# SwiGLU gate and up in Strassen's seven half-size products, with weight sums on GpSimd, in a two-layer encoder trunk

## The chip, the cores and the metric

The kernel runs on one core of one Trainium2 chip. The metric is the device time of one execution in microseconds (us); lower is better. The kernel before takes 2379.37 us (median of 3 runs, 2378.38 to 2380.26).

## The reference

512 tokens of width 1024 go through two layers. Each layer is a half-step SwiGLU, a mixer (gated short convolution beside latent attention), a second half-step SwiGLU and a gated per-layer input; a last RMSNorm follows. All is float32. The part that the change touches is the SwiGLU, of which there are four, each with an inner width of 2816 (22 blocks of 128):

```python
def rmsnorm(x, g):
    y = xf * lax.rsqrt(jnp.mean(xf * xf, axis=-1, keepdims=True) + EPS)
    return (y * g.astype(jnp.float32)).astype(x.dtype)

def swiglu(x, w_gu, w_down):
    g, u = jnp.split(x @ w_gu, 2, axis=-1)
    return (jax.nn.silu(g) * u) @ w_down

for i in range(DEPTH):
    h = h + 0.5 * swiglu(rmsnorm(h, ffn1_norm[i]), ffn1_w_gu[i], ffn1_w_down[i])
    ...
    h = h + merged @ w_o[i]
    h = h + 0.5 * swiglu(rmsnorm(h, ffn2_norm[i]), ffn2_w_gu[i], ffn2_w_down[i])
    ...
```

## The kernel before

**Layout.** The residual stream is eight tiles `h`, each 128 features by 512 tokens. Weights are stationary, activations move. The four SwiGLU stages have the name prefixes a0 and b0 (first layer) and a1 and b1 (second); the mixers are m0 and m1, the per-layer inputs e0 and e1.

**Arithmetic in parts.** Every float32 operand is split into a high part (a cast to fp32r) and a low part (the rest). A product of two tiles takes three matmuls: high by high, high by low, low by high (`mm3`, L155 to L157). A split is a cast on ScalarE and a subtraction on VectorE: for weights L68 and L69 (tiles `wh`, `wl`, 128x1024, eight 128x128 tiles at once), for activations L147/L148, or L150/L151 with the norm's gain folded in.

**Weights.** One DRAM array holds all weight tiles in the order of use. SyncE's queue loads blocks of 16 tiles (1 MB) into three buffers `st`; each block is split in two halves; three buffers each of `wh` and `wl`.

**A SwiGLU stage** (`ffn`). `normed` scales each `h[k]` by the gain, splits it (`x0h`, `x0l`, up to `x7l`) and adds up the squares, on ScalarE and GpSimd (L212 to L216, `acc`). The factor 1/rms is the same for all rows of a token, so the products start without it: `rms` (L225 to L233) multiplies the two parts of `acc` (`ah`, `al`) with ones on TensorE and works out `r` on VectorE (with a reciprocal, L230) and ScalarE (a square root) while the first products run. For each of the 22 blocks f there is a gate product `pg` and an up product `pu`, each 8 x 3 matmuls of 512 columns. Then follow L305 (times r, VectorE from PSUM), L306 (silu, ScalarE), L307 (times r, VectorE), L308 (product of both, GpSimd, or VectorE for the last block of a chunk) and the split. After each chunk of 8, 8 and 6 blocks, eight down products `pd` add that chunk into `h` (L332).

**What sets the order.** The framework puts the instructions of each engine into one fixed list, close to the order of the code, with weight loads and splits moved forward as far as free buffers allow. On the chip each engine works through its list in order and waits at semaphores.

## Time and profile before

| | before |
|---|---|
| timed runs, median (lowest to highest) | 2379.37 us (2378.38 to 2380.26) |
| profiled execution, first to last instruction | 2377.9 us (1.5 us under the median of the runs) |
| mean granted TensorE clock | 0.997 of full speed |
| HBM read, written | 223.66 MB, 2.10 MB |
| first matmuls of a0, b0, a1, b1 start at | 6.8, 771.8, 1186.3, 1944.6 us |
| first matmuls of m0, e0, m1, e1 start at | 369.2, 1131.4, 1546.5, 2304.2 us |

The starts of the stages come from the timeline of TensorE. Each SwiGLU stage thus takes about 360 us. In the profile PE is TensorE's matmuls, PEld its weight loads, DVE VectorE, ACT ScalarE, POOL GpSimd and SP SyncE; a group's row gives its instructions' busy time and the mean of one in nanoseconds, then the idle time of the engine before them and what ended it. L12 is line 12 of the kernel.

### The profile page before, as it was taken

Reading aid. Unit: us, or ns where it says so; the run is one execution under the profiler, and the core shown is the slowest. Engines: PE = TensorE matmul, PEld = TensorE weight load, DVE = VectorE, ACT = ScalarE, POOL = GpSimd, SP = SyncE. Lnnn points to the kernel's source line nnn. Section 1 sums busy time; section 2 is a strip of 40 time slices with the busy share of each in tenths; the row PEclk is TensorE's granted clock in tenths of the full one; section 3 lists DMA queues with packets and bytes.
Section 4 is the critical chain, followed back from the end, with each engine's and each line's share of the span. In section 5 each row is a group of like instructions: output and inputs, shape, how many; then the busy total and the mean of one; then the engine's idle time right before and its main releaser. Section 6 shows DMA issues by size and latency. Waiting matters only on the chain.

```text
span 2377.9 us, 26581 instructions
## 1 busy us (share of the span) xinstructions
PE 2350.9 (99%) x10888; PEld 1967.3 (83%) x10888; DVE 1291.0 (54%) x1735; ACT 832.7 (35%) x1186; POOL 316.2 (13%) x239
## 2 busy tenths in 40 slices
PE   8999999999999999999999999999999999999998
PEld 7888887888888888888888888888888888888888
DVE  6444466754864543435653343467358645444468
ACT  5222234233543322223432222333245333232245
POOL 2000012200222100001310000112012221010011
PEclk9999999999999999999999999999999999999999
DMA  5322222323113232323223232323221132222233
GB/s 178 100 95 93 102 93 89 106 89 101 42 54 107 89 106 89 107 89 115 89 90 106 89 106 89 107 89 107 89 81 47 69 106 89 97 98 91 104 116 124
DMA packets 34537, 227.46 MB, mean 96 GB/s; under 512 B 4080, under 2 KB 4080, under 8 KB 7792
## 3 DMA queue, kind: packets, MB, share of 16 engines
q1 hardware_dynamic: 34128, 225.51, 27.6%
q8 instruction: 85, 1.39, 0.2%
q10 hardware_dynamic: 288, 0.26, 0.0%
q14 instruction: 36, 0.29, 0.0%
HBM read 223.66 MB, written 2.10 MB: 95 GB/s over the span
## 4 chain that ended last, share of the span: by engine, by line
PE 93%; DVE 4%; ACT 1%; issue 1%; POOL 0%; DMA 0%; SPq 0%; ACTq 0%; POOLq 0%; DVEq 0%
PE a0pg L156 2%; PE a0pg L155 2%; PE a1pg L156 2%; PE a0pu L156 2%; PE a0pg L157 2%; PE a0pu L155 2%; PE a0pu L157 2%; PE b1pg L155 2%; PE b1pu L155 2%; PE a1pd L157 2%; PE b0pd L157 2%; PE a1pg L157 2%; PE b0pg L157 2%; PE b0pg L155 2%; PE b0pu L155 2%; PE b0pu L157 2%
## 5 line engine op out<-in xcount | busy, mean ns | idle before, releaser
L69 DVE TENSOR_TENSOR wl<-st,wh 128x1024 fp32r<-128x1024 f32 (+1 forms) x423 | 565.4, 1337 | 392.7 <-ACT wh L68 391.7
L68 ACT CAST wh<-st 128x1024 fp32r<-128x1024 f32 (+1 forms) x423 | 440.8, 1043 | 869.1 <-issue 121.9
L308 POOL TENSOR_TENSOR b0un<-b0un,b0gn 128x512 f32<-128x512 f32 x19 | 25.3, 1333 | 289.4 <-DVE b0un L307 248.7
L308 POOL TENSOR_TENSOR b1un<-b1un,b1gn 128x512 f32<-128x512 f32 x19 | 25.4, 1336 | 288.8 <-DVE b1un L307 250.0
L308 POOL TENSOR_TENSOR a1un<-a1un,a1gn 128x512 f32<-128x512 f32 x19 | 25.3, 1333 | 287.9 <-DVE a1un L307 242.8
L308 POOL TENSOR_TENSOR a0un<-a0un,a0gn 128x512 f32<-128x512 f32 x19 | 25.3, 1333 | 282.1 <-ACT wh L68 166.4
L307 DVE TENSOR_TENSOR a0un<-a0pu,a0r 128x512 f32<-128x512 f32 x22 | 15.2, 690 | 59.5 <-PE a0pu L157 59.5
L307 DVE TENSOR_TENSOR b1un<-b1pu,b1r 128x512 f32<-128x512 f32 x22 | 15.2, 690 | 59.4 <-PE b1pu L157 59.4
L332 DVE SCALAR_TENSOR_TENSOR h<-b1pd,h 128x512 f32<-128x512 f32 x24 | 16.6, 690 | 54.6 <-PE b1pd L157 54.6
L332 DVE SCALAR_TENSOR_TENSOR h<-a0pd,h 128x512 f32<-128x512 f32 x24 | 16.5, 689 | 52.1 <-PE a0pd L157 52.1
L305 DVE TENSOR_TENSOR a0gn<-a0pg,a0r 128x512 f32<-128x512 f32 x22 | 15.2, 691 | 31.5 <-PE a0pg L157 31.4
L305 DVE TENSOR_TENSOR b1gn<-b1pg,b1r 128x512 f32<-128x512 f32 x22 | 15.2, 690 | 31.0 <-PE b1pg L157 31.0
L306 ACT ACTIVATE a1gn<-a1gn 128x512 f32<-128x512 f32 x22 | 13.9, 632 | 47.4 <-DVE a1gn L305 47.4
L306 ACT ACTIVATE b0gn<-b0gn 128x512 f32<-128x512 f32 x22 | 13.9, 632 | 47.4 <-DVE b0gn L305 47.4
L332 DVE SCALAR_TENSOR_TENSOR h<-a1pd,h 128x512 f32<-128x512 f32 x24 | 16.6, 691 | 15.3 <-PE a1pd L157 15.3
L332 DVE SCALAR_TENSOR_TENSOR h<-b0pd,h 128x512 f32<-128x512 f32 x24 | 16.6, 690 | 14.6 <-PE b0pd L157 14.5
L307 DVE TENSOR_TENSOR b0un<-b0pu,b0r 128x512 f32<-128x512 f32 x22 | 15.2, 689 | 10.1 <-PE b0pu L157 10.1
L307 DVE TENSOR_TENSOR a1un<-a1pu,a1r 128x512 f32<-128x512 f32 x22 | 15.2, 689 | 10.1 <-PE a1pu L157 10.1
L430 DVE TENSOR_TENSOR m0gm<-m0gmp,m0r 128x512 f32<-128x512 f32 x8 | 5.5, 692 | 26.4 <-PE m0gmp L157 26.4
L305 DVE TENSOR_TENSOR a1gn<-a1pg,a1r 128x512 f32<-128x512 f32 x22 | 15.2, 690 | 7.7 <-PE a1pg L157 7.7
L305 DVE TENSOR_TENSOR b0gn<-b0pg,b0r 128x512 f32<-128x512 f32 x22 | 15.2, 690 | 7.6 <-PE b0pg L157 7.6
L342 POOL TENSOR_TENSOR m1h0qrt<-m1h0qrt,m1h0qrt 128x512 f32<-128x512 f32 x1 | 2.2, 2236 | 112.9 <-DVE m1h0qrt L341 112.9
(3904 smaller groups left out, 7327.1 us busy)
## 6 DMA issues: line engine op xcount, KB each, us to landing
st<-in_weights SPq DMA_DIRECT2D x208, 1024.0 KB, 4.8
st<-in_weights SPq DMA_DIRECT2D x8, 256.0 KB, 5.4
h<-in_x SPq DMA_DIRECT2D x8, 256.0 KB, 5.4
out<-fo SPq DMA_DIRECT2D x8, 256.0 KB, 2.2
e0pi<-in_p SPq DMA_DIRECT2D x2, 256.0 KB, 5.1
e1pi<-in_p SPq DMA_DIRECT2D x2, 256.0 KB, 5.2
pos_i<-in_positions ACTq DMA_DIRECT2D x1, 256.0 KB, 3.3
cols<-in_gains SPq DMA_DIRECT2D x1, 53.0 KB, 2.0
```

Of the source, the lines that this page charges most:

```text
L68: nc.scalar.copy(hi, src)
L69: nc.vector.tensor_tensor(lo, src, hi.bitcast(F32), ALU.subtract)
L155: nc.tensor.matmul(ps, wh, vh, start=first, stop=False)
L156: nc.tensor.matmul(ps, wh, vl, start=False, stop=False)
L157: nc.tensor.matmul(ps, wl, vh, start=False, stop=last)
L305: nc.vector.tensor_tensor(g, pg, r, ALU.mult)
L306: nc.scalar.activation(g, g, AF.Silu)
L307: nc.vector.tensor_tensor(u, pu, r, ALU.mult)
L308: (nc.vector if last else nc.gpsimd).tensor_tensor(u, u, g, ALU.mult)
L332: nc.vector.scalar_tensor_tensor(h[m], ps, 0.5, h[m], ALU.mult, ALU.add)
L342: nc.gpsimd.tensor_tensor(t1, t1, t2, ALU.add)
L430: nc.vector.tensor_tensor(g, ps, r, ALU.mult)
```

## The change

The gate and up products of two blocks f are seen as a 2 x 2 matrix of weights times a 2 x 2 matrix of activations. The weights' quarters `a11`, `a21`, `a22`, `a12` are (first or second block) by (first or second half of the 1024 features); each holds four tiles of the gate and four of the up, 128x1024 in all. The activations' quarters `b11`, `b12`, `b21`, `b22` are (half of the features) by (half of the tokens, 256). Strassen's method, in Winograd's form, gets the 2 x 2 result in seven products in place of eight. The products are numbered 1 to 7 and run in the order 1, 5, 2, 3, 6, 7, 4; each has 8 tiles x 3 matmuls = 24 matmuls of 256 columns (L400), so 168 of 256 columns for two blocks, where there were 96 of 512.

* **Weight sums** (`Quad.part`): for two blocks s3 = a11 - a21 (L118), a21 + a22 (L119), s2 = that - a11 (L125), a12 - s2 (L126), each 128x1024, on GpSimd (L119 on VectorE in the very first quad). Seven weight splits (L62, L63) for two blocks in place of four.
* **Activation sums** (`halved`): scaling by the gain in halves (L340, first half of the tokens on ScalarE, second on GpSimd), eight sums of 128x512 on VectorE (L356) and fourteen splits (L177, L178), all at the start of a stage.
* **Results**: products 1 and 2 gather in one PSUM bank `a`, 5 and 3 in `c`, 6, 7 and 4 in `b`. Product 1 is copied to SBUF (L427, ScalarE); VectorE makes the sums (L430, L439, L442), multiplies by r (L435 from PSUM, L443 in SBUF) and by the silu (L408 ScalarE, L409 VectorE, 128x256). GpSimd's L308 is gone.
* **Down** in chunks of four blocks (the last of six): from the third pair of blocks on, four down products of 4 x 3 matmuls stand between the seven products of a pair, so 40 updates of `h` (L454) a stage in place of 24.
* **Buffers**: ten of 128x1024 for weights as loaded and for their sums (loads of 512 KB), four for the splits, 62 of 128x512 in one pool that now also holds the squares, the probabilities and their transposes.

```diff
+class Quad:
+    def part(self, j):
+        W = self.W
+        add = W.nc.vector if self.first and j == 5 else W.nc.gpsimd
+        if j == 1:
+            return W.split(self.a11, 512 if self.first else 1024)
+        if j == 5:
+            self.s3 = W.buffer("s3")
+            W.nc.gpsimd.tensor_tensor(self.s3, self.a11, self.a21, ALU.subtract)
+            add.tensor_tensor(self.a21, self.a21, self.a22, ALU.add)
+            return W.split(self.a21)
+        if j == 2:
+            return W.split(self.a12)
+        if j == 3:
+            self.s2 = W.buffer("s2")
+            add.tensor_tensor(self.s2, self.a21, self.a11, ALU.subtract)
+            add.tensor_tensor(self.a12, self.a12, self.s2, ALU.subtract)
+            return W.split(self.a12)
+        return W.split({6: self.s2, 7: self.s3, 4: self.a22}[j])
...
+    def halved(nm, l, name):
...
+        for k in range(KD):
+            for c in range(2):
+                (nc.scalar.mul if c == 0 else nc.gpsimd.tensor_scalar_mul)(
+                    b[k // 2, c][:, k % 2, :], h[k][:, c * H:(c + 1) * H], gain(nm, l, k))
+            sq.add(h[k])
...
+        parts(1, b11)
+        t1 = sums(5, zip(b12, b11))
+        parts(2, b21)
+        parts(3, b22)
+        t2 = sums(6, zip(b22, t1))
+        sums(7, zip(b22, b12))
+        sums(4, zip(b21, t2))
+        return xs, sq.parts()
...
+            product(ps, n, j)
+            if j == 1:
+                d["p1"] = T("p")
+                nc.scalar.copy(d["p1"], ps)
+            if j == 5:
+                d["q"] = T("q")
+                nc.vector.tensor_tensor(d["q"], ps, d["p1"], ALU.add)
+            if n == 0 and j == 2:
+                r.append(rms(acc, D, name))
+            if j == 2:
+                t = T("x")
+                nc.vector.tensor_tensor(t, ps, by_token(0), ALU.mult)
+                activate(n, 0, 0, t)
+            if j == 3:
+                d["w_"] = T("w")
+                nc.vector.tensor_tensor(d["w_"], ps, d["p1"], ALU.add)
+            if j in (6, 7, 4):
+                t, f, c = {6: (d["w_"], 0, 1), 7: (d["q"], 1, 1), 4: (d["p1"], 1, 0)}[j]
+                nc.vector.tensor_tensor(t, ps, t, ALU.add)
+                nc.vector.tensor_tensor(t, t, by_token(c), ALU.mult)
+                activate(n, f, c, t)
...
+        for j in (1, 5, 2, 3, 6):
+            step(0, j)
...
+            order = [(step, n + 1, 1), (step, n, 7), (step, n + 1, 5), (step, n, 4), (step, n + 1, 2), (step, n + 1, 3),
+                     (step, n + 1, 6)]
+            at = {1, 2, 3, 5}
+            for i, (f_, n_, j_) in enumerate(order):
+                f_(n_, j_)
+                if i in at and between:
+                    between.pop(0)()
```

How the lists of the engines change is shown at the start of b0 and in the middle of b0. In these rows `b0x51h` is the high part of the second tile of the operand of product 5, `b00c` bank `c` of pair 0, `b0ah` the high part of the sum of squares, `b0t` a sum of activations, `b0b` a quarter, `s_` a weight sum, and `wl_`, `wh_` the parts of a weight block; a number behind an underscore is that of a buffer.

TensorE at the start of b0, now: the end of product 5, the first matmul of the norm, and the beginning of product 2.

```order
L400 MATMUL b00c<-b0x51h,wh_7123 128x256
L400 MATMUL b00c<-b0x51l,wh_7123 128x256
L400 MATMUL b00c<-b0x51h,wl_7124 128x256
L255 MATMUL b0ps<-b0ah,ones 128x512
L400 MATMUL b00a<-b0x20h,wh_7153 128x256
L400 MATMUL b00a<-b0x20l,wh_7153 128x256
```

The norm's matmul stands ahead of product 2; before, both of the norm's stood behind the fourth product of 24 matmuls of 512 columns.

ScalarE at the same place, now: the last casts of the activations, and the cast on which that matmul waits.

```order
L177 CAST b0x60h<-b0t_7040 128x512
L177 CAST b0x61h<-b0t_7042 128x512
L177 CAST b0x70h<-b0t_7052 128x512
L177 CAST b0x71h<-b0t_7054 128x512
L177 CAST b0x40h<-b0t_7064 128x512
L177 CAST b0x41h<-b0t_7066 128x512
L177 CAST b0ah<-b0acc 128x512
L427 COPY b00p<-b00a 128x512
L62 CAST wh_7307<-s_7120 128x1024
```

The cast of `b0ah` has moved behind the casts of all seven operands, each of which waits for VectorE's sum.

VectorE from the last update of `h` before b0, before the change and then now (first twelve rows; the sums and splits of products 3, 6, 7 and 4 and one more weight split follow).

```order
L562 TENSOR_TENSOR h_96<-m0wop_5587,h_96 128x512
L151 SCALAR_TENSOR_TENSOR b0x7l<-h_96,cols,b0x7h 128x512
L69 TENSOR_TENSOR wl_5752<-st_5720,wh_5751 128x1024
L148 TENSOR_TENSOR b0al<-b0acc,b0ah 128x512
L69 TENSOR_TENSOR wl_5783<-st_5780,wh_5782 128x1024
```

```order
L718 TENSOR_TENSOR h_93<-m0wop_6925,h_93 128x512
L63 TENSOR_TENSOR wl_7202<-st_7086,wh_7201 128x1024
L178 TENSOR_TENSOR b0x10l<-b0b_6957,b0x10h 128x512
L178 TENSOR_TENSOR b0x11l<-b0b_6959,b0x11h 128x512
L356 TENSOR_TENSOR b0t_7012<-b0b_6958,b0b_6957 128x512
L356 TENSOR_TENSOR b0t_7014<-b0b_6960,b0b_6959 128x512
L178 TENSOR_TENSOR b0x50l<-b0t_7012,b0x50h 128x512
L178 TENSOR_TENSOR b0x51l<-b0t_7014,b0x51h 128x512
L178 TENSOR_TENSOR b0x20l<-b0b_6961,b0x20h 128x512
L63 TENSOR_TENSOR wl_7233<-s_7198,wh_7232 128x1024
L178 TENSOR_TENSOR b0x21l<-b0b_6963,b0x21h 128x512
L178 TENSOR_TENSOR b0x30l<-b0b_6962,b0x30h 128x512
```

Before, one subtraction of the activations was left after the last update of `h`; now all 22 rows of sums and splits stand behind it, with two weight splits between them.

GpSimd in the middle of b0, now: the sums of pairs 3 to 6. Before, GpSimd had one product L308 of 128x512 for each block there.

```order
L126 TENSOR_TENSOR st_7764<-st_7764,s_7987 128x1024
L125 TENSOR_TENSOR s_8300<-st_8073,st_8071 128x1024
L118 TENSOR_TENSOR s_8477<-st_8384,st_8386 128x1024
L119 TENSOR_TENSOR st_8386<-st_8386,st_8388 128x1024
L126 TENSOR_TENSOR st_8077<-st_8077,s_8300 128x1024
```

All of its work there is sums of 128x1024 now, four for each pair of blocks.

More of the change, by code (lines that the diff above doesn't have):

```diff
@@ L54, in open @@
[L54 to L71 removed]
+        self.halves = []
```

279 lines of the change are left out of this document (173 added, 106 removed).

## The prediction

> **What bounds the kernel now.** I read the page first: its header, the busy times and the chain that ended last.
>
> ```profile
> span 2377.9 us, 26581 instructions
> PE 2350.9 (99%) x10888; PEld 1967.3 (83%) x10888; DVE 1291.0 (54%) x1735; ACT 832.7 (35%) x1186; POOL 316.2 (13%) x239
> PE 93%; DVE 4%; ACT 1%; issue 1%; POOL 0%; DMA 0%; SPq 0%; ACTq 0%; POOLq 0%; DVEq 0%
> ```
>
> TensorE is busy for 99% of the span and holds 93% of the chain; VectorE is at 54%, GpSimd at 13%. So time goes with the matmuls, as long as nothing makes TensorE wait. The view of waits lists hardly any for it; these are the two longest:
>
> ```profile
> PE a0pg L155 <- ACT a0x0h L150: 6.8, 1, 6.8
> PE m0kvp L156 <- DVE m0x7l L151: 2.1, 1, 2.1
> ```
>
> The first is the kernel's start. No row is for b0, a1 or b1: a SwiGLU stage starts without a hole. The next view, busy time by stretches (columns: stretch, length, then PE, PEld, DVE, ACT, POOL with counts, granted clock, DMA share, GB/s), gives the price of a matmul, in 16 products of b0 and in the end of the kernel, which already has 256 columns:
>
> ```profile
> 902.88:989.92 87.04, 87.04 (x386) 72.10 (x385) 35.52 (x39) 25.53 (x31) 9.01 (x7) 1.00 0.28 97
> 2308.10:2313.62 5.52, 5.52 (x49) 5.52 (x47) 3.15 (x3) 3.15 (x4) 0.15 (x1) 1.00 0.45 174
> ```
>
> The first stretch starts 16 x 24 = 384 matmuls (two more are cut at its edges): 87.04 / 384 = 0.2267 us each. In the second the first and the last start of the timeline are 46 matmuls apart: 5.52 / 46 = 0.1200.
>
> **What the change removes.** Two blocks f cost 96 x 0.2267 = 21.76 before and 168 x 0.1200 = 20.16 now: 1.60 less. Eleven pairs in four stages make 44 x 1.60 = **70.4 us**. The down products keep their matmuls: four between the products of a pair are 48 x 0.2267 = 10.88, so a pair with them lasts 31.04 of TensorE, one without 20.16. A half-size matmul thus costs more than half (0.1200 against 0.1133). The Trainium skill (TensorE: Matmul & The Clock Gate, "Back-to-back issue gap") has columns / 2.4 GHz + 2.5 ns for a lone warm matmul, 215.8 and 109.2 ns; by it the saving would be 44 x (20.72 - 18.35) = 104 us, an estimate. Both rows lie 11 ns above it, so this trace disagrees.
>
> **What the change adds on VectorE and GpSimd.** Prices, from the groups and from the timeline (columns: start, length, engine, line, operation):
>
> ```profile
> L307 DVE TENSOR_TENSOR a0un<-a0pu,a0r 128x512 f32<-128x512 f32 x22 | 15.2, 690 | 59.5 <-PE a0pu L157 59.5
> L308 POOL TENSOR_TENSOR b0un<-b0un,b0gn 128x512 f32<-128x512 f32 x19 | 25.3, 1333 | 289.4 <-DVE b0un L307 248.7
> L609 DVE TENSOR_TENSOR e_256g<-e1gp,e1r 128x256 f32<-128x256 f32 x8 | 3.4, 420 | 3.4 <-PE e1gp L157 3.3
> L230 DVE RECIPROCAL b0r<-b0t 128x512 f32<-128x512 f32 x1 | 3.4, 3353 | 0.7 <-ACT b0t L229 0.7
> L68 ACT CAST wh<-st 128x1024 fp32r<-128x1024 f32 x415 | 435.9, 1051 | 867.2 <-issue 121.9 <-PE b1pu L156 78.3 <-PE b1pd L156 69.7
> L503 POOL TENSOR_SCALAR m1s20e<-m1s20e,m1s20sm 128x384 f32<-128x384 f32 x1 | 1.2, 1244 | 1.2 <-DVE m1s20sm L498 1.2
> 1192.60 1.21 DVE L69 TENSOR_TENSOR wl<-st,wh 128x1024 fp32r<-128x1024 f32 x1
> 1193.73 0.74 DVE L151 SCALAR_TENSOR_TENSOR a1x6l<-h,cols,a1x6h 128x512 fp32r<-128x512 f32 x1
> 1194.40 0.74 DVE L151 SCALAR_TENSOR_TENSOR a1x7l<-h,cols,a1x7h 128x512 fp32r<-128x512 f32 x1
> ```
>
> Where VectorE's rows follow each other without a wait they start 1.13 (1024) and 0.66 (512) apart, a little less than they last; I take these, and 0.40 for 256. A GpSimd sum of 128x1024 is not in the trace. The row of 512 is the lower bound, 1.33, twice that the upper, 2.67. GpSimd's time goes with the elements (a row of 384 takes 1.24), so the price is near the upper end; I take 2.36.
>
> The two engines get in each other's way:
>
> ```profile
> 60.19 1.23 DVE L69 TENSOR_TENSOR wl<-st,wh 128x1024 fp32r<-128x1024 f32 x1 [0.22 <-ACT wh L68]
> 65.55 1.28 POOL L308 TENSOR_TENSOR a0un<-a0un,a0gn 128x512 f32<-128x512 f32 x1 [8.36 <-DVE a0un L307]
> 65.61 2.30 DVE L69 TENSOR_TENSOR wl<-st,wh 128x1024 fp32r<-128x1024 f32 x1 [0.21 <-ACT wh L68]
> 1114.57 1.73 POOL L216 TENSOR_TENSOR e0acc<-e0acc,e0sq 128x512 f32<-128x512 f32 x1 [4.21 <-ACT e0sq L215]
> 1115.24 0.69 DVE L332 SCALAR_TENSOR_TENSOR h<-b0pd,h 128x512 f32<-128x512 f32 x1
> ```
>
> The weight subtraction, both inputs in SBUF, takes 1.23 alone and 2.30 beside a GpSimd row of 1.28: it gains 1.07 for 1.22 of overlap, 84% or more. The update of `h`, one input in PSUM, keeps its 0.69. The Trainium skill (SBUF — State Buffer, "Who interferes with whom") says that whoever starts first keeps the shared port for its whole instruction, and the other stands still. By that, four sums would take 9.4 us a pair from VectorE; by the row it is 4 x 2.36 x 0.84 = 7.9, which I use.
>
> *A pair with down products.* VectorE has 9 weight splits, 15 rows of 512 and 4 of 256: 10.2 + 9.9 + 1.6 = 21.7, with the sums 29.6, under TensorE's 31.04. ScalarE: nine casts at 1.05 and some small rows, about 13. So TensorE stays the bound, narrowly: cost nothing, upper bound 1.5 us a pair in 32 pairs where waits bunch.
>
> *A pair without them* (the first two of a stage): 7 splits, 11 rows of 512, 4 of 256: 16.8, with the sums 24.7 against 20.16. TensorE waits 4.5 us a pair.
>
> *The start of b0 and b1.* Before, from the last matmul of w_o, 771.82:
>
> ```profile
> 772.02 0.69 DVE L562 TENSOR_TENSOR h<-m0wop,h 128x512 f32<-128x512 f32 x1 [0.59 <-PE m0wop L157]
> 772.75 0.72 ACT L150 ACTIVATE b0x7h<-h,cols 128x512 fp32r<-128x512 f32 x1 [2.58 <-DVE h L562]
> 773.38 0.62 ACT L215 ACTIVATE b0sq<-h 128x512 f32<-128x512 f32 x1
> 775.53 0.61 ACT L147 CAST b0ah<-b0acc 128x512 fp32r<-128x512 f32 x1
> ```
>
> Only one block of `h` is late, and it is needed last. Now the scaling of the last block and its square stand ahead of the first cast in ScalarE's list: h at 0.9 us after the last matmul, scaling 0.4, square 0.6, cast 0.6, so VectorE starts its chain at 2.55. Product 1 (24 x 0.12 = 2.88) and product 5 then run. Ahead of product 2 stands the norm's matmul, which waits for `b0ah`, which waits behind the casts of all operands, the last of which waits for VectorE's last sum: 20 rows at 0.66 and 2 at 1.13, 15.5, ends at 18.0; two casts, 19.3. By then TensorE has worked 5.8: **13.5 lost**. Product 2 and the norm end at 22.4; 0.7 for `ms`, 0.6 root, 3.4 reciprocal, then 4 weight splits, 6 rows of 512, one of 256 (8.9) until L442 has read bank b: product 7 starts at 36.1. Seven products are 20.2: 15.9 lost. In this phase four sums come, as buffers are freed by the splits: up to 9.4 more, 25.3. The rest of the two pairs without down, some 1.5, adds 7: 32. The idle stretch also costs clock. In the one stage start that waited (m0, whose waits are above), the clock fell:
>
> ```profile
> 375.00:382.00 7.00, 3.70 (x9) 2.73 (x10) 5.11 (x4) 4.03 (x7) 2.87 (x4) 0.67 0.08 32
> ```
>
> 0.67 of full over 7 us loses about 2. So 34 lost against 17.6 saved a stage: **+17 each for b0 and b1**.
>
> *a1.* Here e0 comes before, and its last matmul ends at 1186.3:
>
> ```profile
> 1181.11 1.29 POOL L612 TENSOR_TENSOR h<-h,e_0g 128x512 f32<-128x512 f32 x1 [3.90 <-DVE e_0g L611]
> 1188.96 0.68 DVE L612 TENSOR_TENSOR h<-h,e_0g 128x512 f32<-128x512 f32 x1
> ```
>
> The last block of `h` is there 3.4 after the last matmul, 2.5 later than in b0; the one before it is GpSimd's, and GpSimd's eight scalings (128x256, 0.9 by the row of 384 columns) and seven sums of squares (1.3) now stand behind that update in its list: 16.5 in all, of which some 8 fall into VectorE's chain and hold its rows up by 84%, 7 us. 17 + 2.5 + 7: **+26**.
>
> *a0.* Data arrive like this:
>
> ```profile
> 0.00:5.00 5.00, 0.00 (x0) 0.00 (x0) 0.46 (x5) 1.90 (x3) 0.68 (x6) 1.00 0.56 114
> 5.00:10.00 5.00, 3.25 (x7) 2.29 (x8) 3.41 (x5) 4.22 (x9) 0.99 (x1) 1.00 1.03 383
> 10.00:15.00 5.00, 5.00 (x19) 4.03 (x18) 5.00 (x4) 5.00 (x11) 3.96 (x4) 1.00 1.07 403
> ```
>
> Now 14 loads of 256 KB (a11, a21, a22, all of `h`), 3.7 MB, must land before the first cast: 0.6 + 1.9 + 3.0 x 0.4 puts that at 13. Behind it GpSimd does one scaling, two sums of squares and three weight sums (10.6, with the port shared some 17) before the split of product 3, which stands in the middle of VectorE's chain; 12 more rows' worth and two casts bring product 2 to about 42: 36 lost, and 20 after it. Before, the 96 matmuls of the first four products (21.8) were through at 31.4, so 10 were lost:
>
> ```profile
> 31.38 0.40 PE L225 MATMUL a0ps<-a0ah,ones 128*128 128x512 f32 x1
> ```
>
> 36 + 20 - 10 - 17.6 = **+29**.
>
> *End of a stage*: the last split waits for six short rows, 3.5, beside a down part of 12 x 0.2267 = 2.7: 0.8 x 4 = **+3**.
>
> The mixers and per-layer inputs keep their matmuls; that their tiles share one pool I take as nothing (their other work hides it).
>
> **Sum** against the profiled execution: 2377.9 + 2 x 17 + 26 + 29 + 3 = 2470; the runs' median lies 1.5 above: **2471 us**. The 70.4 saved are in it, 162 are lost.
>
> **Rivals.**
> (A) GpSimd's sums fall into VectorE's waits and cost nothing. For: VectorE waits often for PSUM. Against: at the start it does not wait. Then b0 and b1 lose 18 each, a1 20, a0 40: 2379 + 96 - 10 - 70 = 2395.
> (B) The pairs with down products bunch: 29.6 of 31.04 leaves little, and a row that blocks VectorE also delays casts. 32 x 1.5 = 48 more: 2520.
> (C) Faster: the start is paid by less than 17.6 us a stage, the point from which the change wins. Place: the norm's matmul ahead of product 2. If the chain's rows pass at 0.45, since sums and subtractions alternate and ScalarE keeps pace, each stage loses 11 to 13, a0 20: 2379 + 57 - 10 - 70 = 2356. Against it: no row of 512 from SBUF starts less than 0.6 after the last.
> (D) The change does not save what it says: 256-column matmuls with fresh weights each. Against: the stretch shown has a load for each matmul (47 beside 49) and still 0.1200. No time of its own.
>
> **Chances.** Forecast 0.50, A 0.20, B 0.20, C 0.10. The range goes from A's time less the error of the walk through the list to B's with the sum at its upper price: 2390 to 2540. A measurement here tells 0.2% (5 us) from no change: faster 0.09, same 0.03, slower 0.88.
>
> **What would show it.** In the trace after: matmuls of 256 columns 0.12 apart within a product; in b0 a hole of TensorE of 9 to 12 us ended by ScalarE's `b0ah`, and a second one ended by VectorE's L442; weight splits beside sums of over 2 us; pairs 3 to 9 of 31 to 32 us each. I am wrong in the main step if the holes at the stage starts come to less than 70 us in all, or if pairs with down products last over 33.

## The result, and the profile after

| | before | after |
|---|---|---|
| timed runs, median (lowest to highest) | 2379.39 us (2378.38 to 2380.26), 4 runs | 2517.02 us (2515.55 to 2518.27), 4 runs |
| after / before, 95% interval | | 1.0578, [1.0563, 1.0593] |
| profiled execution, first to last instruction | 2377.9 us | 2515.9 us |
| mean granted TensorE clock | 0.997 | 0.969 |

The change makes the kernel 138 us (5.8%) slower. The page of after: header, busy times, granted clock and TensorE's busy share in 40 slices, the costliest groups.

```profile
span 2515.9 us, 34779 instructions
PE 2328.7 (93%) x14056; PEld 2094.2 (83%) x14056; DVE 1800.4 (72%) x2372; ACT 1024.8 (41%) x1504; POOL 693.6 (28%) x370
PE   3899999999999599999949999999999977999997
PEclk9999999999999799999979999999999988999998
L63 DVE TENSOR_TENSOR wl<-st,wh 128x1024 fp32r<-128x1024 f32 (+1 forms) x465 | 634.8, 1365 | 289.7 <-ACT wh L62 288.0
L118 POOL TENSOR_TENSOR s<-st,st 128x1024 f32<-128x1024 f32 x44 | 112.3, 2553 | 633.8 <-DVE wl L63 633.8
```

TensorE was busy for 99% of a shorter span and is now at 93%; the idle slices (62.9 us each) are the first, the 14th, the 21st, the 33rd with the 34th, and the last: where a0, b0, a1 and b1 start, and the end. The clock row falls in the same places but the first. VectorE rose from 54% to 72%, GpSimd from 13% to 28%: neither is a bound by its average. The view of waits of after (TensorE; line waited for, us in total, times, longest) says what ends the idle time:

```profile
PE a00a L400 <- ACT a0x10h L177: 16.7, 1, 16.7
PE a0ps L255 <- ACT a0ah L177: 15.8, 1, 15.8
PE b10b L400 <- DVE b10w L442: 13.1, 1, 13.1
PE a10b L400 <- DVE a10w L442: 13.0, 1, 13.0
PE b00b L400 <- DVE b00w L442: 12.9, 1, 12.9
PE a1ps L255 <- ACT a1ah L177: 12.0, 1, 12.0
PE b0ps L255 <- ACT b0ah L177: 10.4, 1, 10.4
...
PE b00a L400 <- ACT b0x10h L177: 7.0, 1, 7.0
...
PE fss L792 <- POOL f0acc L246: 2.5, 1, 2.5
```

Each of b0, a1 and b1 starts with three holes: product 1 waits for the first cast of its operands (`b00a`), the norm's matmul ahead of product 2 for the cast of the squares' sum (`b0ps`), product 7 for VectorE's reading of bank b (`b00b`). The view's fourteen longest, all at the starts of the four SwiGLU stages, add up to 143 us.

A table by stage, from the first matmul starts in the traces (a0 from the span's start; m0 and m1 to the last matmul of w_o; b0 and b1 from there to e0 or e1; a1 from the last matmul of e0; e1 to the first of the last group of transposes). The column "forecast" is what the prediction's sum puts on each stage.

| stage | before | after | difference | forecast |
|---|---|---|---|---|
| a0 | 369.2 | 409.6 | +40.4 | +29.8 |
| m0 | 402.4 | 407.5 | +5.1 | 0 |
| b0 | 359.8 | 384.7 | +24.9 | +17.8 |
| e0 and a1 | 415.2 | 441.5 | +26.3 | +26.8 |
| m1 | 397.9 | 400.3 | +2.4 | 0 |
| b1 | 359.8 | 384.5 | +24.7 | +17.8 |
| e1 and the end | 66.5 | 80.6 | +14.1 | 0 |
| all | 2370.8 | 2508.6 | +138 | +92 |

The start of b0 in the timeline (start, length, engine, line, operation; in brackets the idle time before it). The last matmul of w_o starts at 817.0; times "after w_o" are counted from there, 0.2 earlier than in the prediction.

```profile
819.48 2.33 POOL L126 TENSOR_TENSOR st<-st,s 128x1024 f32<-128x1024 f32 x1
...
821.85 1.04 ACT L62 CAST wh<-st 128x1024 fp32r<-128x1024 f32 x1 [6.26 <-POOL st L126]
822.80 0.50 ACT L340 ACTIVATE b0b<-h,cols 128x256 f32<-128x256 f32 x1
823.73 0.60 ACT L177 CAST b0x10h<-b0b 128x512 fp32r<-128x512 f32 x1
...
843.12 0.69 DVE L178 TENSOR_TENSOR b0x41l<-b0t,b0x41h 128x512 fp32r<-128x512 f32 x1
843.65 0.79 PE L255 MATMUL b0ps<-b0ah,ones 128*128 128x512 f32 x1 [10.42 <-ACT b0ah L177]
...
849.98 0.69 DVE L258 TENSOR_SCALAR b0ms<-b0ps 128x512 f32<-128x512 f32 x1 [4.98 <-PE b0ps L256]
...
857.42 3.43 DVE L63 TENSOR_TENSOR wl<-st,wh 128x1024 fp32r<-128x1024 f32 x1
860.77 2.84 DVE L262 SCALAR_TENSOR_TENSOR b0t<-b0t,b0ms 128x512 f32<-128x512 f32 x1
863.53 3.35 DVE L63 TENSOR_TENSOR wl<-st,wh 128x1024 fp32r<-128x1024 f32 x1
...
873.59 0.69 DVE L442 TENSOR_TENSOR b00w<-b00b,b00w 128x512 f32<-128x512 f32 x1
```

Read it as three steps. ScalarE stands still for 6.26 us: the cast of product 3's weights is ahead of the last scaling in its list, and those weights come from GpSimd's sum L126. So product 1 starts 7.4 us after w_o. VectorE then makes the operands of all seven products (from 824.3 to 843.8), and only behind them comes the cast for which the norm waits. And between the norm (849.98) and L442 (873.59) VectorE has 24 us of reciprocal, weight splits and sums; two splits and a row of 512 columns are stretched to 3.43, 3.35 and 2.84 beside GpSimd's sums (1.22 and 0.68 alone). A comparison of three windows (columns: stretch, length, busy PE, PEld, DVE, ACT, POOL, granted clock, DMA share, GB/s) gives what the holes do to the clock:

```profile
844.30:849.40 5.10, 5.10 (x25) 5.10 (x25) 0.70 (x2) 0.00 (x0) 0.00 (x0) 0.50 0.00 0
850.00:856.00 6.00, 6.00 (x52) 6.00 (x51) 5.33 (x4) 3.81 (x5) 0.00 (x0) 1.00 0.28 87
215.41:246.50 31.09, 31.09 (x218) 29.13 (x217) 23.78 (x28) 12.54 (x16) 9.79 (x4) 1.00 0.33 102
```

Behind the 10.42 us wait, 5.1 us of matmuls run at half the clock (25 in 5.1 us; at full clock 52 in 6.0 us). The third row is a whole pair of blocks with down products in a0: 31.09 us, no hole. Away from the starts the change does what it says.

### The profile page after: what moved, and what is told of

Same layout as the page of the kernel before. It is cut to its first block, busy times and chain, and to the rows that moved or that the text cites. A ratio compares the mean times of both kernels' runs of the same rounds, so it can differ in the third digit from the quotient of the medians.

```text
span 2515.9 us, 34779 instructions
## 1 busy us (share of the span) xinstructions
PE 2328.7 (93%) x14056; PEld 2094.2 (83%) x14056; DVE 1800.4 (72%) x2372; ACT 1024.8 (41%) x1504; POOL 693.6 (28%) x370
## 5 line engine op out<-in xcount | busy, mean ns | idle before, releaser
L63 DVE TENSOR_TENSOR wl<-st,wh 128x1024 fp32r<-128x1024 f32 (+1 forms) x465 | 634.8, 1365 | 289.7 <-ACT wh L62 288.0
L62 ACT CAST wh<-st 128x1024 fp32r<-128x1024 f32 (+1 forms) x465 | 486.7, 1047 | 841.9 <-issue 135.8
L118 POOL TENSOR_TENSOR s<-st,st 128x1024 f32<-128x1024 f32 x44 | 112.3, 2553 | 633.8 <-DVE wl L63 633.8
L125 POOL TENSOR_TENSOR s<-st,st 128x1024 f32<-128x1024 f32 x44 | 109.8, 2495 | 164.3 <-DVE wl L63 156.8
L126 POOL TENSOR_TENSOR st<-st,s 128x1024 f32<-128x1024 f32 x44 | 107.6, 2446 | 121.7 <-issue 61.5
L63 DVE TENSOR_TENSOR wl<-s,wh 128x1024 fp32r<-128x1024 f32 x88 | 107.0, 1216 | 6.8 <-ACT wh L62 6.6
L119 POOL TENSOR_TENSOR st<-st,st 128x1024 f32<-128x1024 f32 x43 | 110.3, 2566 | 3.3
L62 ACT CAST wh<-s 128x1024 fp32r<-128x1024 f32 x88 | 91.8, 1043 | 38.6 <-PE b00a L400 6.8
L454 DVE SCALAR_TENSOR_TENSOR h<-b0pd,h 128x512 f32<-128x512 f32 x40 | 27.2, 682 | 4.0 <-PE b0pd L187 4.0
L454 DVE SCALAR_TENSOR_TENSOR h<-b1pd,h 128x512 f32<-128x512 f32 x40 | 27.2, 682 | 4.0 <-PE b1pd L187 4.0
L454 DVE SCALAR_TENSOR_TENSOR h<-a1pd,h 128x512 f32<-128x512 f32 x40 | 27.2, 682 | 3.8 <-PE a1pd L187 3.8
L454 DVE SCALAR_TENSOR_TENSOR h<-a0pd,h 128x512 f32<-128x512 f32 x40 | 27.2, 681 | 1.8 <-PE a0pd L187 1.8
L246 POOL TENSOR_TENSOR m0acc<-m0acc,m0sq 128x512 f32<-128x512 f32 x7 | 12.7, 1807 | 50.9 <-ACT m0sq L245 50.9
L246 POOL TENSOR_TENSOR e0acc<-e0acc,e0sq 128x512 f32<-128x512 f32 x7 | 10.7, 1530 | 47.0 <-ACT e0sq L245 46.7
```

The lines of the kernel that those rows point to most:

```text
L62: self.nc.scalar.copy(hi[:, w], src[:, w])
L63: self.nc.vector.tensor_tensor(lo[:, w], src[:, w], hi[:, w].bitcast(F32), ALU.subtract)
L118: W.nc.gpsimd.tensor_tensor(self.s3, self.a11, self.a21, ALU.subtract)
L119: add.tensor_tensor(self.a21, self.a21, self.a22, ALU.add)
L125: add.tensor_tensor(self.s2, self.a21, self.a11, ALU.subtract)
L126: add.tensor_tensor(self.a12, self.a12, self.s2, ALU.subtract)
```

## The experiments

Lengths of the stages in all runs, cut as above; "half rate" is what matmuls lost that started 1.7 to 2.35 times their full-clock spacing apart, counted over the whole timeline. The cuts of the edits are against after in runs 1 to 4, against run 3 in run 5, against the run before in runs 6 to 11, and against before in run 12.

| run | us | ratio to before, 95% interval | a0 | m0 | b0 | a1 | m1 | b1 | e1 | half rate |
|---|---|---|---|---|---|---|---|---|---|---|
| before | 2379.4 | | 369.2 | 402.4 | 359.8 | 360.5 | 397.9 | 359.8 | 66.5 | 6.3 |
| after | 2517.0 | 1.0578 [1.0563, 1.0593] | 409.6 | 407.5 | 384.7 | 386.7 | 400.3 | 384.5 | 80.6 | 33.9 |
| 1 | 2488.6 | 1.0457 [1.0441, 1.0472] | 406.5 | 406.9 | 374.4 | 382.3 | 400.4 | 374.3 | 80.7 | 31.1 |
| 2 | 2440.0 | 1.0249 [1.0232, 1.0267] | 383.3 | 404.4 | 369.1 | 375.4 | 396.3 | 368.2 | 80.6 | 29.3 |
| 3 | 2477.5 | 1.0409 [1.0394, 1.0425] | 405.3 | 406.8 | 371.2 | 382.8 | 398.8 | 369.3 | 79.3 | 23.1 |
| 4 | 2494.5 | 1.0478 [1.0462, 1.0494] | 408.9 | 408.5 | 380.5 | 386.4 | 400.6 | 380.4 | 66.9 | 31.4 |
| 5 | 2459.2 | 1.0337 [1.0320, 1.0354] | 401.3 | 406.1 | 370.9 | 380.8 | 397.0 | 369.4 | 69.6 | 24.5 |
| 6 | 2434.5 | 1.0234 [1.0217, 1.0251] | 394.5 | 407.4 | 364.3 | 374.7 | 397.0 | 364.4 | 68.1 | 24.2 |
| 7 | 2463.4 | 1.0351 [1.0333, 1.0368] | 395.1 | 420.8 | 367.8 | 375.6 | 404.0 | 366.1 | 70.3 | 33.0 |
| 8 | 2398.8 | 1.0081 [1.0064, 1.0098] | 390.5 | 409.6 | 356.8 | 356.7 | 397.3 | 355.5 | 68.5 | 21.9 |
| 9 | 2383.4 | 1.0016 [1.0006, 1.0026] | 383.9 | 396.3 | 357.0 | 357.7 | 396.3 | 357.8 | 69.6 | 20.4 |
| 10 | 2348.9 | 0.9871 [0.9855, 0.9888] | 373.4 | 400.2 | 347.7 | 352.0 | 396.3 | 347.7 | 69.6 | 12.3 |
| 11 | 2376.1 | 0.9986 [0.9976, 0.9996] | 368.3 | 401.0 | 359.8 | 359.8 | 396.3 | 359.8 | 66.7 | 4.0 |
| 12 | 2389.5 | 1.0043 [1.0028, 1.0058] | 368.4 | 402.0 | 361.1 | 362.8 | 397.5 | 367.0 | 66.4 | 6.6 |

**1. Only the cast of the squares' sum goes ahead of the operands.** In after's `halved`:

```diff
+        acc = sq.parts()
         b11, b12, b21, b22 = (...)
...
-        return xs, sq.parts()
+        return xs, acc
```

> Moves the cast of the sum of squares ahead of the operands' casts; nothing else. My theory (the order of ScalarE's list is what product 2 waits for): the four waits for the norm's cast (b0ah 10.4, b1ah 10.4, a1ah 12.0, a0ah 15.8) go, product 2 of b0 starts about 10 us earlier after the last w_o matmul than the 27 us of the changed kernel. But the norm's row ms, its root and reciprocal still stand behind the operand chain on VectorE, so product 7 gains only the 5 to 7 us in which VectorE stood still: 4 x 6 = 24 less, 2493 (2480 to 2505). Rival (VectorE's total work bounds the start, the wait only moves to L442): 2510 to 2517, with the holes before bank b longer by what the others lost.

Measured 2488.6, 28.4 saved. The four waits of the norm's matmul are gone, but product 2 starts at 29.7 us after w_o, and not 10 us earlier than the 27.2 of after.

```profile
PE a00a L401 <- ACT a0x10h L177: 30.1, 1, 30.1
PE a10a L401 <- ACT a1x10h L177: 18.6, 1, 18.6
...
PE b00a L401 <- ACT b0x10h L177: 9.1, 1, 9.1
```

```profile
833.12 0.39 PE L401 MATMUL b00b<-b0x60h,wh 128*128 128x256 f32 x1 [1.07 <-ACT b0x60h L177]
...
843.14 0.41 PE L401 MATMUL b00a<-b0x20h,wh 128*128 128x256 f32 x1
```

The rows of the first block (the view of waits) show that part of the wait has moved to product 1: the first operand's cast now stands behind that of the squares' sum, which waits for GpSimd (16.7, 7.0 and 7.0 in after). Those of the second (the timeline) show that product 2 starts without a wait: TensorE's list now has product 6 and the next pair's product 1 ahead of it. So the edit moved more than the one cast. Product 7 comes 10 us earlier (47.3 against 57.3), as the factor r is there sooner. All told this place in the list costs 28 us net, not the start's whole loss.

**2. The four weight sums of each pair left out.** The weights of products 5, 3, 6 and 7 are then a21, a12, a21 and a11 as loaded; splits and matmuls stay.

```diff
-        if j == 5:
-            self.s3 = W.buffer("s3")
-            W.nc.gpsimd.tensor_tensor(self.s3, self.a11, self.a21, ALU.subtract)
...
+        return W.split({5: self.a21, 3: self.a12, 6: self.a21, 7: self.a11, 4: self.a22}[j])
```

> Leaves the four GpSimd sums per pair out (products 5, 3, 6 and 7 use the raw quarters a21, a12, a21 and a11), so the output is another one. My theory (the sums cost only where VectorE or ScalarE is the bound): each stage start loses 4.6 less for the cast that waits for the sum at L126 and 4 to 9 less for splits beside sums, pairs 0, 1 and 11 some 4 less each; pairs 3 to 9 stay at 31.1: 4 x (4.6 + 7 + 8) = 78 less, 2440 (2425 to 2465). Rival A (the sums fall into waits and cost nothing): 4 x 4.6 = 18 less, 2498 (2490 to 2517). Rival B (they cost in every pair with down products): pairs 3 to 9 below 31.0 is impossible for TensorE, so this rival can only show as pairs that were over 31.1 and now are not.

Measured 2440.0. All 176 sums cost 77 us, and the table says where: a0 26.3, a1 11.3, b0 15.6, b1 16.3, m0 3.1, m1 4.0. A pair with down products starts 31.1 us after the one before, with the sums (first row, after) and without (second row, this run), and VectorE's busy time (third number of busy time) hardly differs, 23.80 and 22.21:

```profile
945.32:976.44 31.12, 31.12 (x218) 29.16 (x217) 23.80 (x29) 12.44 (x16) 9.79 (x4) 1.00 0.32 103
...
897.56:928.68 31.12, 31.12 (x218) 29.16 (x217) 22.21 (x28) 12.64 (x17) 0.00 (x0) 1.00 0.32 102
```

So the sums cost time at the stage starts and none in the steady part. In the mixers one wait of 1.6 us at w_o's last block (for `m0mg7h` and `m1mg7h`) is there with the sums and gone without. With them all gone the kernel is still 61 us slower than before: the larger share of the start's loss is not the weight sums'.

**3. Operands made block by block as `h` comes in; the norm's cast ahead of the last group.**

```diff
+        for j in range(2):
+            scaled(2 * j, 2 * j + 1)
+            parts(1, j, b11[j])
+            t1.append(sums(5, j, b12[j], b11[j]))
+        for j in range(2):
+            scaled(2 * j + 4, 2 * j + 5)
+            if j:
+                acc = sq.parts()
+            parts(2, j, b21[j])
...
```

> The same operand rows in another order: those of h0 to h3 (products 1 and 5) are emitted as soon as these blocks are updated, then those of h4 and h5, then those of h6 and h7, and the norm's cast ahead of the last group. My theory (the start is lost to the order of the lists, since h0 to h6 are ready 5 to 38 us before w_o ends): only some 13 rows of VectorE, the norm's 6.7 us and the splits remain behind the last block; product 7 of b0 starts near 32 us after the last w_o matmul in place of 57; b0, b1 and a1 gain 25 each, a0 15: 2427 (2405 to 2450). Rival (VectorE's total work and its port bound the start, whatever the order): less than 40 us gained, 2480 to 2515.

Measured 2477.5: a miss by 50, and 39.5 gained, the rival's "less than 40". Product 1 now starts at 0.2 us after w_o, but the norm's matmul still waits 8.0 us and starts at 14.1, and product 2, behind product 6 and the next pair's product 1 as in run 1, at 26.0. GpSimd's rows of this run's timeline, at the start of b0, show why the norm waits:

```profile
817.51 2.72 POOL L126 TENSOR_TENSOR st<-st,s 128x1024 f32<-128x1024 f32 x1 [2.40 <-DVE wl L63]
...
821.44 1.91 POOL L341 TENSOR_SCALAR b0b<-h,cols 128x256 f32<-128x256 f32 x1
823.33 2.22 POOL L246 TENSOR_TENSOR b0acc<-b0acc,b0sq 128x512 f32<-128x512 f32 x1
```

The last scaling and the last sum of squares stand behind a weight sum in GpSimd's list, and both take about twice their time beside VectorE (0.91 and 1.25 in a0 of after). I had moved VectorE's work and left GpSimd's.

**4. Squares in a pool of their own** (`acc` two tiles, `sq` three; the big pool 57 tiles in place of 62).

```diff
-            sq = G(self.name + "sq")[:, :w]
+            sq = qp.tile([P, S], F32, tag="sq", name=self.name + "sq", bufs=3)[:, :w]
```

> Undoes one part of the change: the squares and their sum get their own small pool again (57 + 5 buffers in place of 62). In ScalarE's list at the end of e1 one square then no longer stands behind the two copies of the transposed blocks, as in the kernel before. My theory (that place in the list made e1 14 us longer): e1 goes from 88.0 back to 75 or 76, the rest moves by less than 5: 2505 (2498 to 2511). Rival (e1 lost by the clock or by splits that are prefetched deeper): e1 stays within 3 us of 88, 2515.

Measured 2494.5, under the expected 2498 to 2511. The last stage goes from 80.6 to 66.9: 13.7 of the 14.1 us lost there came from the one pool. In after, ScalarE's list of that stage has the first square of the last norm behind the copies of the output:

```profile
2469.30 0.58 ACT L806 COPY fu<-ft 128x512 f32<-128x512 f32 x1 [2.85 <-PE ft L803]
...
2470.57 0.43 ACT L245 ACTIVATE f0sq<-h 128x256 f32<-128x256 f32 x1
```

With tiles of their own the squares move ahead of them (2450.28 to 2453.34, the copies from 2455.51). The edit touches pools alone, so a change of pools can change an engine's list. It did so in b0 and b1 too, which the theory did not foresee: product 1 of b0 starts at 0.2 us after w_o and not at 7.4. Only 4.2 and 4.1 us of that arrive, since the norm's matmul then waits 10.8.

**5. Both together, and more:** sums of the first pair ahead of the stage, the last scalings on ScalarE, sums of activations in place, and the norm's matmul given out ahead of the last operands.

```diff
+            quad(0)
+            todo[0]["w"].sum5()
+            todo[0]["w"].sum3(True)
...
-                acc = sq.parts()
+                r = rms(sq.parts(), D, name)
```

> The order of e3 and the pool of e4 together, and the queues cleared: the four sums of a stage's first pair are emitted ahead of its operand rows (GpSimd is idle while w_o runs), the scalings and the adding of squares of h6 and h7 go to ScalarE and VectorE, the operands' sums are written in place, the norm is emitted ahead of the last operand rows, the gates of the per-layer input get two buffers of their own, so that a1's first tiles need not wait for e0's last. My theory (the start holes are a matter of which row stands ahead of which in the lists of GpSimd, ScalarE and VectorE): product 7 of b0 starts near 30 us after the last w_o matmul (57 in the changed kernel, 44 in e3); b0 and b1 last 350, a1 355, a0 ends near 385, e1 67; half-rate stretches fall by half: 2376 (2360 to 2400), about the kernel before. Rival (port and VectorE's total work): b0 stays over 365 and the whole over 2430.

Measured 2459.2, a miss by 83. The view of waits names my own edit: the norm's matmul now stands first in TensorE's list, ahead of product 1.

```profile
PE a0ps L268 <- ACT a0ah L190: 42.0, 1, 42.0
PE a1ps L268 <- ACT a1ah L190: 20.6, 1, 20.6
```

**6. The norm given out behind products 1 and 5;** in a0 TensorE adds the squares itself.

```diff
+            if j == 2:
+                r.append(rest())
             step(0, j)
```

> e5 with two places moved, and a third: the norm is emitted behind products 1 and 5 in place of ahead of them (in e5 TensorE's list had its matmul first, and TensorE stood 10.2 us in b0 and b1, 20.6 in a1 and 42.0 in a0 for its cast); the rotary angles, whose rows stand among VectorE's rows at the end of a0, are emitted later; in a0 the squares are added by TensorE (eight matmuls in fp32 with the ones) and ScalarE does the scalings of h4 to h7, so that GpSimd has only the weight sums. My theory (order alone): b0 and b1 begin at once and lose no more than 8 us at the start, 350 and 350; a1 360; a0 ends near 375; m0 loses its 5 us of waits at the start: 2400 (2380 to 2420). Rival (in e5 the cast was late because VectorE, GpSimd and the port have no more to give; then the wait only moves to product 2, 6 or 7): 2445 to 2460.

Measured 2434.5, between the theory and the rival. Product 2 starts 7.9 us after w_o, yet product 7 at 37.7, with 6.9 to 8.2 us of waiting at L472 (after's L442): the first pair needs 20 us of TensorE and, as I read it, more of VectorE, in whatever order.

**7. The first pair in eight full-size products** as before the change, and the operands of the seven made under them; the rotary tables moved to just ahead of m0's scores. The sums that run 5 made ahead of the stage are back in their old place, and TensorE no longer adds the squares.

```diff
-        xs, rest = halved(nm, l, name, first)
+        x8, acc = normed(nm, l, name)
+        pss = [PS(f"{name}p{w}{f}") for f in range(2) for w in "gu"]
...
+        xs = halved(nm, l, name, x8)
+        r.append(rms(acc, D, name))
```

> Undoes one part of the change, with the pools of e5: the first pair of blocks of each stage is computed in eight full products again, from operands of 512 columns as in the kernel before (products 1, 2 and 3 then use halves of these operands, and only the operands of 5, 6, 7 and 4 need sums); Strassen's products begin with the second pair, whose operands and the norm are made beside the first pair's 21.8 us of TensorE; the rotary angles are emitted later in m0. My theory (all of the loss but 14 us is the start of the stages; pairs from the third on keep the saving of 1.60): ten pairs in four stages save 64, the starts lose 2 to 3 us each as before the change, e1 is as in e4, m0 as before: 2379 - 64 + 4 x 3 + 4 + 4 = 2335 (2320 to 2360), faster than the kernel before. Rival (the clock or VectorE's load take back what a pair saves, wherever the stage begins): 2365 to 2400.

Measured 2463.4, a miss by 128. Two waits of this run: m0 (420.8) waits in its scores, ahead of which the rotary tables now stand, and the second pair waits for its weights (some 25 us in the four stages). They explain less than half of the miss.

```profile
PE m0s00p L654 <- ACT m0h0qn0h L178: 22.1, 1, 22.1
...
PE b01b L411 <- ACT wh L62: 6.0, 1, 6.0
```

**8. As 7, with the sums of the second pair made ahead into buffers of their own, and the operands of product 5 block by block.**

```diff
+        def sums_first():
+            quad(1)
+            todo[1]["w"].sum5()
+            todo[1]["w"].sum3(True)
```

> e7 with its lists cleared: the four weight sums of the second pair are emitted ahead of the stage's operand rows, the last of them into a buffer of its own (in e7 ScalarE stood for it, 6 to 7 us of TensorE's time per stage, since it waits for the split of product 2 and stood behind a sum of the third pair); product 5's operands are made block by block beside w_o; the rotary angles move ahead of the gates (in e7 their chain stood just ahead of the first scores, 22.1 us of TensorE's time). My theory (order alone, VectorE has room for the rest beside 21.8 us of full products): b0 and b1 350, a1 356, a0 375, m0 404, m1 398, e0 54.7, e1 70: 2350 (2330 to 2375), faster than the kernel before. Rival (VectorE's rows at a stage's start are too many in any order): b0 and b1 over 360, 2400 or more.

Measured 2398.8. Three SwiGLU stages are now shorter than before the change (b0 356.8, a1 356.7, b1 355.5 against about 360), while a0 is at 390.5 and m0 at 409.6, where the rotary tables sit in yet another place.

**9. Two pairs in eight products, the rotary tables in the middle of a0.** `p2 = block(2)` and `p3 = block(3)` are written out, `step(1, j)` becomes `step(2, j)`. The same edit moves `rest(x8)`, which makes the operands of products 6, 7 and 4, from ahead of the norm to behind it, and the weight sums behind the first pair.

> e8 with the first two pairs of each stage in eight full products (43.5 us of TensorE), Strassen's from the third pair on, so that the operands of 6, 7 and 4, the norm and the sums have twice the time beside them; the rotary angles are made in the middle of a0. My theory (VectorE's rows of the start fit when they have 43 us of full products beside them, and the rest of the loss in e8 is a0, which lost 35 us against its TensorE time, and 10.5 us of m0 for the angles): nine pairs in four stages save 58; a0 360, m0 402, b0 348, e0 54.7, a1 349, m1 397, b1 348, e1 67: 2336 (2322 to 2355), faster than the kernel before. Rival (a0 is bound by loading and by the port whatever is computed first; the pairs in seven products lose their saving again where they begin): a0 over 380, b0 over 355, 2380 or more.

Measured 2383.4, 0.16% above before. The mixers are mended (396.3); b0, a1 and b1 stand where they stood in 8. Two things moved at once here, the second pair and the operands of products 6, 7 and 4, which run 8 had made ahead of the norm; run 10 takes the second back.

**10. Those operands ahead of the norm,** a0's operands of product 5 behind its eight blocks, the rotary tables beside m0's first projections.

```diff
+        rest(x8)
         r.append(rms(acc, D, name))
...
-        rest(x8)
```

> e9 with three places moved: the operands of products 6, 7 and 4 are emitted ahead of the norm (VectorE stands idle for some 20 us until the norm's matmul comes behind the first pair), in a0 the operands of product 5 come behind the eight blocks of x and not between them, and the rotary angles stand beside the first projections of m0. My theory (order alone): the waits of e9 at the first Strassen pair (2.3 + 1.6 and the half rate behind them, some 6 us per stage) and 9 us of a0 go, m0 stays at 396: b0, a1, b1 350 to 352, a0 372: 2352 (2340 to 2365), faster than the kernel before by 1%. Rival (the waits move to the next list): over 2375.

Measured **2348.9 us (2348.49 to 2351.38), 1.3% faster than before the change** and by the medians 6.7% faster than after. Its page and three windows, all in b0 (its first pair, the stretch behind the start of the seven products at 817.8, and 240 us of the middle):

```profile
span 2349.2 us, 33482 instructions
PE 2306.3 (98%) x13480; PEld 2048.5 (87%) x13480; DVE 1738.2 (74%) x2338; ACT 998.9 (43%) x1453; POOL 565.1 (24%) x303
...
774.00:795.70 21.70, 21.70 (x97) 17.99 (x96) 18.40 (x24) 9.16 (x14) 4.08 (x3) 1.00 0.29 91
...
820.00:840.00 20.00, 18.67 (x153) 18.38 (x153) 17.88 (x21) 10.01 (x14) 3.10 (x2) 1.00 0.41 132
...
840.00:1080.00 240.00, 240.00 (x1657) 224.37 (x1656) 181.60 (x216) 94.86 (x123) 70.90 (x29) 1.00 0.32 104
```

In the first row TensorE works through a pair of full-size products while VectorE, 18.40 of 21.70 busy, makes operands. The one hole left near the start is 1.3 us, and then TensorE has none in 240 us. Runs 8 and 10 both make these operands ahead of the norm: with one pair in eight b0 takes 356.8, with two 347.7 (the weight sums also stand in another place). With two pairs and the operands behind the norm, run 9, it takes 357.0. So b0 needs these operands ahead of the norm and, as it seems, the second pair too.

**11. As 10, without the seven products:** all pairs in eight, down in chunks of four, same buffers.

```diff
-        for j in (1, 5, 2, 3, 6):
-            step(2, j)
+        for n in range(2, np_ - 1):
+            f0, m0 = (n - 2) // 2 * 4, 4 * (n % 2)
...
```

> e10 with Strassen's products taken out: all eleven pairs of each stage in eight full products, no weight sums, no operands of 5, 6, 7 and 4; the pools, the down products in chunks of four, the place of the rotary angles and all else as in e10. My theory (the saving of 1.60 per pair is real wherever its start is covered, and it is what makes e10 faster): nine pairs in four stages are 57.6 of TensorE's time, less some 12 that e10 still loses where Strassen's products begin: 2349 + 57.6 - 12 = 2394 (2380 to 2405), not faster than the kernel before. Rival (e10's gain comes from the down products in chunks, the pools or the angles, not from the seven products): 2345 to 2365.

Measured 2376.1. So 3.3 us of 10's gain come from the other changes of place and 27.2 from the seven products: b0 and b1 12.1 each and a1 7.8 less, a0 5.1 and e1 2.9 more. (These stages sum to 24 by the two profiled executions.) By the number of matmuls nine pairs are worth 14.4 a stage, 57.6 in all; about half arrives. Most of what is missing is a0's: 19.5 us, of which the timelines show 11.7 as waits behind the first one and 4.6 at half rate that run 11 does not have. In a1 one wait of 3.8 and 1.7 at half rate make up 5.5 of the missing 6.6.

**12. In the kernel before, chains of multiplications by 1.0 on VectorE,** meant to make TensorE wait at seven places without any other change.

```diff
+            for _ in range(delay.get((name, f), 0)):
+                nc.vector.tensor_scalar(u, u, 1.0, None, ALU.mult)
```

> The kernel before with seven waits put in: in b0, a1 and b1 a block that the next down product needs is multiplied by 1.0 on VectorE 7, 9, 12 (b0), 14, 19, 24 (a1) and 33 times (b1) before its split, so that TensorE should wait some 1 to 12 us at seven places that have no wait now. My theory (the clock is lowered by the waits alone, so that the term of 2 us a stage in the prediction was too small only because the holes were longer and more): behind a wait of under 1 us no half rate, behind one of 2 to 4 us some 3 to 7 us of it (2 to 3.5 us lost), behind longer ones 7 to 14 us (3.5 to 7 lost); the waits sum to about 25 and the half rate adds some 15: 2420 (2405 to 2435). Rival (the half rate of the changed kernel belongs to the 256-column matmuls or the load of the port): the clock stays at full rate, 2400 to 2405 for the waits alone.

Measured 2389.5, under the expected 2405 to 2435: a row of these chains takes 0.46 us where I had counted 0.66, and other work covers most of it. One long wait is left, and it shows the effect in a kernel that has no half-size matmul:

```profile
PE b1pd L155 <- ACT b1a7h L147: 4.2, 1, 4.2
...
2054.20:2058.20 4.00, 4.00 (x10) 3.08 (x10) 2.37 (x4) 2.94 (x3) 0.00 (x0) 0.50 0.00 0
```

Behind a wait of 4.2 us, at least 4 us at half rate: some 2 us more. How the loss grows with the wait is not settled by one point.

## Why the prediction was right, and where it was not

The sign, the place and the kind of loss were right: the holes at the four stage starts decide, and 2517 lies in the range. In b0 the two holes that were named came, 10.4 us ended by `b0ah` and 12.9 ended by L442; the third, ahead of product 1, is 7.0 us, where the forecast had product 1 start at 2.6. The forecast was +92 and +138 came: most terms of loss were too small, and some too dear. By its own steps:

* **The saving, 70.4.** Right as far as the traces show it: a pair with down products is 31.09 us (31.12 from start to start), forecast 31.04. The figure of the Trainium skill for a lone matmul (TensorE: Matmul & The Clock Gate, "Back-to-back issue gap"), by which an estimated 104 would have been saved, is not borne out.
* **Pairs without down products.** 24.7 us were forecast, 4.5 above TensorE's own 20.16; in b0 of after the fourth pair starts 21.5 us behind the third, 1.4 above, and in run 2, without the weight sums, 20.2. The step was too dear because the toll of the sums was: the forecast let four sums take 7.9 us from VectorE in each pair. In a steady pair VectorE's own rows were priced well (21.7, and run 2 has 22.2), but the sums add 1.6 to them and not 7.9 (23.8 in all, forecast 29.6). As I read it, most of GpSimd's 9.8 us there fall where VectorE waits or reads PSUM; no run separates this.
* **The start of b0 and b1, +17 each, measured +25.** Three terms were too small. By the prediction's zero: *product 1* was to start at about 2.6 and starts at 7.1. The step missed stands in ScalarE's list, not in VectorE's: the cast that waits 6.26 us for L126. *The norm's matmul* was to start at 19.3 and starts at 26.4: 4.5 from that late start and 2.6 because VectorE's rows up to its last sum take 18.1 us and not 15.5 (they come 0.60 apart and not 0.66, but the two weight splits among them wait 2.2 us for their casts). In run 4, where only pools were changed, product 1 starts at 0.2, so the cast's place in the list came with the one pool; but b0 gains only 4.2 by it. *Product 2 with the norm* takes 6.3, not 3.1: half rate. *From `ms` to product 7* it takes 24.4 us, forecast 13.7 + 9.4 = 23.1, which held. So product 7 starts at 57.1 and not at 45.5. All told b0 lost 17.6 + 24.9 = 42.5 us: 30.3 in the three holes, 2.8 in small waits, 6.2 at half rate; 3.2 I cannot place.
* **The clock, 2 us a stage, 8 in all.** Of the starts' terms this was furthest off. Half rate costs 33.9 us in after and 6.3 before, so 27.6 more, 22.5 of it in the four SwiGLU stages. I had sized it by one window behind one wait; three waits a stage each bring a stretch of their own (6.2 in b0 by the timeline). Run 12 shows by one case that a wait is enough, without half-size matmuls; in run 10, with most of the holes gone, it falls to 12.3.
* **a1, +26:** 26.3 came (with e0), but by luck. It was to lose 9.5 more than b0, for the late last block and for GpSimd's scalings; it lost 1.3 more. What b0's terms were short of made up for that.
* **a0, +29: +40.** The two waits ahead of product 1 are 16.7 and 5.7, more than the 13 us of loading allowed. VectorE's one weight sum, which stands in its list ahead of the low part of product 1's first operand, waits for its load until 20.0:

```profile
20.01 2.27 DVE L119 TENSOR_TENSOR st<-st,st 128x1024 f32<-128x1024 f32 x1 [10.75 <-DMA st<-in_weights]
```

The norm's matmul ahead of product 2 starts at 55.4, where product 2 was to start at about 42.
* **Mixers and e1, "I take as nothing": 21.6 us.** 14.1 of it are the last stage, and run 4 shows the one pool as the cause (13.7). That term, put at nothing without a row behind it, is 22.5 us in all by run 4. In the mixers, 5.1 and 2.4, the sums are behind most of it: without them (run 2) the loss is gone in m1 and 3.1 smaller in m0.

Of the rivals, A (sums cost nothing) falls with run 2: they cost 77 us. B's time was nearly met, but by other means: pairs with down products did not bunch (31.1 apart). C named the right place, and run 1 puts 28 us net on it, too little to win. D is refuted by the pair's 31.09.

What the experiments add: most of the loss at the starts was avoidable. What made the seven products lose was that the stage began with them. Eight activations' worth of sums must be made before the first pair, when TensorE has nothing else; with two pairs in eight products as cover, and the norm behind the operands, the same idea wins 1.3%. What a0 would need to get its share of the 57.6 us I did not try; it and e1 gave back 8.

## What to carry to other kernels

A scheme that trades matmuls for additions needs its additions made while something else feeds TensorE: keep the old form for the first blocks of each stage as cover (here two pairs; with one, b0 took 9 us longer), and change over behind it. Before you price a new chain on one engine, walk through every engine's list at that place, casts of weights included, since a cast that waits for another engine blocks whatever stands behind it. Price a new hole with the slow stretch behind it, and a changed buffer pool with the order that it sets.

## What the runs showed of the hardware

* **A wait can be paid twice.** Behind waits of 4.2 (run 12) and 10.4 us (after) TensorE ran 4 to 5 us at a granted clock of 0.50; behind the waits of 0.3 to 0.7 us in run 12's a1 no matmul at half rate follows. Run 10 narrows it: the clock stays at 1.00 behind a wait of 1.33 us (first row) and is 0.50 behind one of 1.91 (second row).

```profile
825.04:828.00 2.96, 2.96 (x24) 2.96 (x25) 2.96 (x3) 0.89 (x1) 2.73 (x1) 1.00 0.32 127
...
60.40:63.60 3.20, 3.20 (x17) 3.20 (x16) 2.51 (x4) 1.50 (x3) 1.82 (x1) 0.50 0.03 8
```

How the length of the stretch depends on the wait stays open.
* **A weight split nearly stands still beside a GpSimd sum.** In b0 of after a weight split takes 3.43 us beside a GpSimd sum, and 1.22 alone:

```profile
856.99 2.78 POOL L118 TENSOR_TENSOR s<-st,st 128x1024 f32<-128x1024 f32 x1 [31.71 <-DVE wl L63]
...
870.80 1.22 DVE L63 TENSOR_TENSOR wl<-st,wh 128x1024 fp32r<-128x1024 f32 x1 [2.58 <-ACT wh L62]
```

The split starts at 857.42, the sum ends at 859.77: 2.35 us of overlap cost 2.21, or 94%. The forecast's row of before, by the same measure, has 88% (1.07 of 1.22; its 84% is of GpSimd's whole row), and it took 1.98 us for a sum. The measured 94% is closer to what the Trainium skill (SBUF — State Buffer, "Who interferes with whom") says, that the engine which comes second is blocked until the other's instruction is through.
* **A GpSimd sum of 128x1024** takes 2.33 us where nothing is beside it (819.48 above), as estimated (2.36); the means of the four groups in after, many of them with VectorE beside them, are 2.45 to 2.57.
